# The expert weights of a dense loop in whole rows: two loads of 4096 bytes a partition instead of four of 2048

## The chip, the cores and the metric

The kernel runs on one core of a Trainium2 chip, in one launch. The metric is the device time of that launch in microseconds (us); of several runs the median is taken. The engines are TensorE (PE; its weight loads are listed as PEld), VectorE (DVE), ScalarE (ACT), GpSimd (POOL) and SyncE (SP); each works off its own list of instructions in a fixed order, and transfers are done by 16 DMA engines, which the instructions of SP and POOL feed.

## The reference

One decoder layer for 512 tokens of 1024 features: a sparse attention and a gated linear recurrence side by side, an output projection, LayerNorm, and then a layer that retrieves experts ("PEER"), LayerNorm again. The change lies in the PEER layer:

```python
def _peer(x, w_q, sub_keys, u, v):        # u, v: 16384 experts of 1024 floats each
    def one_block(xb):                    # 128 tokens
        q = (xb @ w_q).reshape(PEER_BLOCK, PEER_HEADS, 2, PEER_KEY_DIM // 2)
        s = jnp.einsum('thpd,hpkd->thpk', q, sub_keys).astype(jnp.float32)
        ...
        g = jax.nn.softmax(best, axis=-1).astype(xb.dtype)        # 8 heads, 16 experts each
        h = jax.nn.gelu(jnp.einsum('td,thkd->thk', xb, u[experts]))
        return jnp.einsum('thk,thkd->td', g * h, v[experts])
...
x = _layer_norm(ALPHA * h + ffn, ln2_g[layer], ln2_b[layer])
```

## The kernel before

The 512 tokens are four blocks of 128. Blocks 0 and 1 fetch the 128 experts of each token by indirect transfers (L627 on POOL, a ring `g` of four tiles, rows of 4096 bytes), and DVE multiplies and sums them (`gu` at L651, `gv` at L664). Blocks 2 and 3 ("dense") compute all 16384 experts for their 256 tokens, with a matrix `G` that holds each token's weight for each expert, zero for those not chosen.

`dense` first builds `G`: for four tokens at a time DVE writes two tiles of one-hot rows (`og`, L735), ACT multiplies the weights into one of them, PE multiplies the two (`gb`, L744) and ACT copies the product into `G` (L722). Then block 0 is finished: `finish(0)` does the LayerNorm of its accumulator in place (L143, L144) and stores it (L641).

The dense loop has 129 turns; turn j treats group j of 128 experts and the output side of group j - 1. In a step stand
- `into_hidden(j, n)`, for halves n = 0 and 1 of the features: a load of half of `u_j` (L767), and `split`: ACT rounds it to `u_nh` (L760), DVE subtracts to get the rest `u_nl` (L762); three times four matmuls add to `hp` (L771);
- `weigh`: the activation of `hp` gives `w` on ACT (L776), DVE multiplies in `G` (L777), then `wh` (ACT, L779) and `wl` (DVE, L781);
- `out_of_hidden(j - 1, n)`: a load of half of `v` (L786), `split` into `v_nh` and `v_nl`, and six matmuls for each half that add to `acc` (L791);
- `pump`: about two rows of experts of block 1 (one POOL transfer and one DVE instruction L651 or L664 each).

In turn 2, `residual` adds the layer's input to `acc` by 64 matmuls (L800); in turn 127, `finish(1)` ends block 1; after the loop the LayerNorm of blocks 2 and 3 and their store follow (L830).

The u halves have a ring of four tiles of 2 KB a partition, the v halves one of three, the split halves (`hl`) one of six. A load is issued by SP when its tile's last reader is done. The order of instructions on each engine is fixed when the program is built, by a scheduler that estimates when each could run; it is not the order of the text, and a change in tiles can move instructions of other engines.

Of the kernel before, what the change touches and what calls it, by code (L numbers as in the profile page):

```python
# [9 lines left out]
F32 = mybir.dt.float32  # L10
# [14 lines left out]
DENSE = (2, 3)  # L25
# buffers of the rings of tiles
HGB = 5
GB = 4
UB = 4
VB = 3  # L30
HLB = 6
# [3 lines left out]
# rows of experts worked off at each such place of the program (sel: one at every second step)  # L35
PUMP = {"cw": 4, "qi": 4, "hf": 4, "hq": 4, "hi": 4, "hg": 3, "qa": 2, "hgrn": 1, "att": 4, "mix": 1, "sel": 2,
        "q0": 7, "q1": 0, "q2": 0, "q3": 0}
# rows of block 0's sum that the tensor engine takes: after the queries, and beside the dense weights
# [4 lines left out]
# tokens of each four whose weights ScalarE multiplies in  # L43
GACTS = (3, 4)
# a row of experts at every so manyth group of the dense weights
GPUMP = 3
# the dense step by which all rows are worked off
# [4 lines left out]
def tile_decoder_layer(ctx, tc, a, out):  # L52
    nc = tc.nc

    cst = ctx.enter_context(tc.tile_pool(name="cst", bufs=1))
# [67 lines left out]
    def layer_norm(ys, os_, g, b, nm):  # L123
        """Each y is a tile or a list of its parts along the features."""
        n = len(ys)
        mv = cst.tile([128, n, 2], F32, name="mv" + nm, tag="ln_mv", bufs=2)
        parts = [y if isinstance(y, list) else [y[:, k * 512:(k + 1) * 512] for k in range(2)] for y in ys]
        for i in range(n):
            st = cst.tile([128, 2, 6], F32, name=f"st{nm}_{i}", tag="ln_st", bufs=2)
            for k in range(2):  # L130
                nc.vector.bn_stats(st[:, k, :], parts[i][k])  # L131
            nc.vector.bn_aggr(mv[:, i, :], st)
        ve = cst.tile([128, n], F32, name="ve" + nm, tag="ln_ve", bufs=2)
        nc.vector.tensor_scalar(ve, mv[:, :, 1], EPS, None, op0=ALU.add)
        r = rsqrt(ve, n, nm)
        for i, o in enumerate(os_):
            if isinstance(ys[i], list):
                for k in range(2):
                    sl = slice(k * 512, k * 512 + 512)
                    nc.vector.scalar_tensor_tensor(o[:, sl], parts[i][k], mv[:, i, 0:1], g[:, sl],  # L140
                                                   op0=ALU.subtract, op1=ALU.mult)
            else:
                nc.vector.scalar_tensor_tensor(o, ys[i], mv[:, i, 0:1], g, op0=ALU.subtract, op1=ALU.mult)  # L143
            nc.vector.scalar_tensor_tensor(o, o, r[:, i:i + 1], b, op0=ALU.mult, op1=ALU.add)  # L144
# [24 lines left out]
    hsA = cst.tile([128, 2, 1024], F32, name="hsA")  # L169
    hsB = cst.tile([128, 2, 1024], F32, name="hsB", tag="hsB")  # L170
    hTh = cst.tile([128, 8, 256], F32R, name="hTh")
    hs = [hsA[:, 0, :], hsA[:, 1, :], hsB[:, 0, :], hsB[:, 1, :]]
# [6 lines left out]
    def tok_major(blocks, xT, w, name):  # L179
        """x W for each block, tokens on partitions."""  # L180
# [12 lines left out]
    def feat_major(blocks, xT, w, name):  # L193
        """(x W)^T for all blocks at once, features on partitions: a bank for each 128 features."""
# [23 lines left out]
    def lower_bound():  # L218
# [7 lines left out]
        # lower bound of the forget gate: f = fa + fc * tanh(z / 2)  # L226
# [42 lines left out]
    def hgrn(b, pr, mixT):  # L269
# [42 lines left out]
        # the states before each chunk of 32  # L312
# [87 lines left out]
    def select(b, pr):  # L400
        """What to add to the negated attention scores of the keys that the index doesn't choose."""
# [91 lines left out]
    def queries(blocks, hT):  # L493
        """Sub-key scores and, for each of the 16 lists, its 16 best."""
# [54 lines left out]
    def best16(b, g, sv, si, bv, pos):  # L549
        # a pair (a, b) can be among the 16 best only if (a + 1) * (b + 1) <= 16; the places keep the pairs' order  # L550
# [16 lines left out]
    def routing(b, half, sv, si, bv, pos):  # L567
        """The experts and their weights for four of the block's heads."""
        H = slice(half * 4, half * 4 + 4)
        C = slice(half * 64, half * 64 + 64)  # L570
        # place -> the two ranks
# [22 lines left out]
        # rank -> sub-key  # L594
# [21 lines left out]
        # softmax over the 16 kept, whose first is their maximum  # L616
# [28 lines left out]
    def peer_gather(b):  # L645
        """Yields True after each row of experts is worked off, False where it waits for pe_gather."""
# [25 lines left out]
    def pe_gather(n, p):  # L672
        """A part of block 0's sum over the rows of v on the tensor engine: diag(weight) @ rows; yields after each."""
# [28 lines left out]
    def dense(den, dps):  # L702
        """Tokens of the DENSE blocks against every expert, with the experts' weights scattered to a dense matrix."""
# [4 lines left out]
        for i, b in enumerate(DENSE):  # L708
# [3 lines left out]
            t = den.tile([128, 4, 128], F32, name=f"dtr{b}", tag="v", bufs=VB)  # L712
            nc.scalar.copy(t[:, 0:3, :].rearrange("p a b -> p (a b)"), p[:, :384])
            tr[b] = [t[:, n, :] for n in range(3)]
# [13 lines left out]
        for t0 in range(0, T, 4):  # L728
# [3 lines left out]
            og = [den.tile([128, 4, 128], F32, name=f"og{t0}_{n}", tag=tag, bufs=bufs)  # L732
                  for n, (tag, bufs) in enumerate((("u", UB), ("hl", HLB)))]
# [30 lines left out]

        def into_hidden(j, n, hp):
            u = den.tile([128, 512], F32, name=f"u{j}_{n}", tag="u", bufs=UB)
            nc.sync.dma_start(u.rearrange("p (k i) -> p k i", k=4), a["ut"][j, :, n * 4:n * 4 + 4, :])  # L767
            uh, ul = split(f"u{j}_{n}", u)
# [15 lines left out]
        def out_of_hidden(j, n, wh, wl):  # L784
            v = den.tile([128, 512], F32, name=f"v{j}_{n}", tag="v", bufs=VB)
            nc.sync.dma_start(v, a["v"][j * 128:(j + 1) * 128, n * 512:(n + 1) * 512])  # L786
            vh, vl = split(f"v{j}_{n}", v)
# [15 lines left out]

        due = 0
# [124 lines left out]
```

## Time and profile before

| | |
|---|---|
| median of 3 runs | 1659.23 us (1658.19 to 1664.06) |
| span of the profiled execution, first to last instruction | 1647.0 us |
| its own time beside the span | not listed by itself; the median is 12.2 us above the span |
| PE busy | 1456.9 us (88%) |
| DVE busy | 1387.7 us (84%) |
| ACT busy | 706.5 us (43%) |
| POOL busy | 663.7 us (40%) |
| DMA moved | 467.89 MB, mean 284 GB/s |

The shares are means over the whole span. The building of `G` ends and the dense loop begins at about 880 us and the loop goes on to about 1634 us, so the loop is nearly half of the time. How the stages differ is in the rows below.

### The profile page before, as it was taken

How to read it: one execution, taken by the hardware profiler on the slowest of the kernel's cores; microseconds unless marked ns; L12 is line 12 of the kernel's file. 1: busy time of each engine (PE TensorE's matmuls, PEld its weight loads, DVE VectorE, ACT ScalarE, POOL GpSimd, SP SyncE). 2: the span in 40 equal slices, each digit the busy share in tenths (PEclk: the TensorE clock that was granted, in tenths of full speed). 3: DMA queues.
4: the chain of work that ended last, by engine and by line, in shares of the span. 5: the costliest groups of instructions: out<-in, count | busy, mean ns of one | idle time of the engine just before them, and what ended most of it. 6: DMA issues, size and time to landing. Idle time of an engine off the chain costs nothing. (4 is left out here: it accounts for less than half of the span.)

```text
span 1647.0 us, 24505 instructions
## 1 busy us (share of the span) xinstructions
PE 1456.9 (88%) x7858; PEld 1096.3 (67%) x7858; DVE 1387.7 (84%) x3263; ACT 706.5 (43%) x1501; POOL 663.7 (40%) x531
## 2 busy tenths in 40 slices
PE   8889899763577899868998999999999999999996
PEld 4567444542333365425667888888888889989885
DVE  4139899787787669998887899998999899999998
ACT  3312321122233010327996555555555555555553
POOL 0003423456665251135443344443444345534540
PEclk9899899755599999989999999999999999999998
DMA  7377878788887785246677999999999999999995
GB/s 284 122 275 248 280 265 290 245 273 275 262 276 252 264 306 186 84 136 226 220 218 263 327 345 351 355 345 344 343 356 344 336 347 359 365 349 345 354 358 191
DMA packets 166161, 467.89 MB, mean 284 GB/s; under 512 B 18576, under 2 KB 18704, under 8 KB 165904
## 3 DMA queue, kind: packets, MB, share of 16 engines
q0 software_dynamic: 73728, 268.47, 48.0%
q1 hardware_dynamic: 92304, 197.86, 33.2%
q8 instruction: 62, 1.02, 0.2%
q14 instruction: 67, 0.55, 0.1%
HBM read 464.16 MB, written 2.10 MB: 283 GB/s over the span
## 5 line engine op out<-in xcount | busy, mean ns | idle before, releaser
L627 POOL DMA_INDIRECT gv<-in_v_dram,idx x256 | 335.1, 1309 | 420.0 <-DVE hsA L664 268.6
L627 POOL DMA_INDIRECT gu<-in_u_dram,idx x256 | 318.6, 1245 | 458.2 <-DVE gu L651 289.3
L651 DVE SCALAR_TENSOR_TENSOR gu<-gu,hsA 128x1024 f32<-128x1024 f32 x256 | 309.5, 1225 | 52.5 <-DMA gu<-in_u_dram,idx 51.9
L664 DVE SCALAR_TENSOR_TENSOR hsA<-gv,gate,hsA 128x1024 f32<-128x1024 f32 x204 | 261.6, 1282 | 30.0 <-DMA gv<-in_v_dram,idx 26.6
L760 ACT CAST v_0h<-v 128x512 fp32r<-128x512 f32 x128 | 79.7, 622 | 96.7 <-PE acc L791 55.4
L518 PE MATMUL pq<-hT,wpq 128*128 128x128 f32 (+1 forms) x512 | 118.8, 390 | 0.0
L760 ACT CAST v_1h<-v 128x512 fp32r<-128x512 f32 x128 | 79.5, 621 | 88.6 <-DMA v<-in_v_dram 45.7
L762 DVE TENSOR_TENSOR u_0l<-u,u_0h 128x512 fp32r<-128x512 f32 x128 | 88.5, 692 | 32.7 <-ACT u_0h L760 29.9
L760 ACT CAST u_0h<-u 128x512 fp32r<-128x512 f32 x128 | 79.4, 620 | 72.2 <-PE hp L771 40.1
L791 PE MATMUL acc<-v_0h,wl 128*128 128x512 f32 x256 | 101.9, 398 | 2.5 <-DVE wl L781 2.5
L518 PEld LDWEIGHTS pq<-hT,wpq 128*128 128x128 f32 x512 | 80.0, 198 | 32.1 <-issue 1.7
L762 DVE TENSOR_TENSOR v_1l<-v,v_1h 128x512 fp32r<-128x512 f32 x128 | 87.8, 686 | 15.8 <-ACT v_1h L760 13.5
L791 PE MATMUL acc<-v_0h,wh 128*128 128x512 f32 x256 | 101.0, 394 | 0.0
L791 PE MATMUL acc<-v_1h,wl 128*128 128x512 f32 x256 | 99.7, 389 | 0.0
L791 PE MATMUL acc<-v_1h,wh 128*128 128x512 f32 x256 | 99.7, 389 | 0.0
L791 PE MATMUL acc<-v_0l,wh 128*128 128x512 f32 x256 | 99.5, 390 | 0.0
L760 ACT CAST u_1h<-u 128x512 fp32r<-128x512 f32 x128 | 79.4, 621 | 46.4 <-PE acc L791 42.3
L735 DVE TENSOR_TENSOR og<-iota,dtr 128x512 f32<-128x512 f32 x128 | 81.6, 687 | 13.6 <-PE gb L744 11.7
L762 DVE TENSOR_TENSOR u_1l<-u,u_1h 128x512 fp32r<-128x512 f32 x128 | 87.8, 686 | 5.1 <-ACT wh L779 2.7
L762 DVE TENSOR_TENSOR v_0l<-v,v_0h 128x512 fp32r<-128x512 f32 x128 | 88.0, 688 | 3.4 <-ACT v_0h L760 2.1
L682 PE MATMUL pw<-gv,dg 128*128 128x512 f32 x152 | 76.0, 623 | 15.6 <-ACT dg L680 9.1
L771 PE MATMUL hp<-hTl,u_0h 128*128 128x256 f32 x512 | 84.3, 287 | 5.8 <-ACT u_0h L760 5.8
(282 smaller groups left out, 3166.6 us busy)
## 6 DMA issues: line engine op xcount, KB each, us to landing
v<-in_v_dram SPq DMA_DIRECT2D x256, 256.0 KB
u<-in_ut_dram SPq DMA_DIRECT2D x256, 256.0 KB
wpq<-in_w_pq_dram SPq DMA_DIRECT2D x32, 512.0 KB
wo<-in_w_o_dram SPq DMA_DIRECT2D x16, 512.0 KB
hfw<-in_w_hf_dram SPq DMA_DIRECT2D x8, 512.0 KB
hqw<-in_w_hq_dram SPq DMA_DIRECT2D x8, 512.0 KB
hiw<-in_w_hi_dram SPq DMA_DIRECT2D x8, 512.0 KB
qaw<-in_w_qa_dram SPq DMA_DIRECT2D x8, 512.0 KB
```

The costliest lines, as they stand in the source:

```text
L518: nc.tensor.matmul(qp[:, :nt], w[:, k, :], hT[:, k, :nt], start=(k == 0), stop=(k == 7))
L627: nc.gpsimd.indirect_dma_start(out=t, out_offset=None, in_=table, in_offset=bass.IndirectOffsetOnAxis(ap=idx[b][k // 64][:, k % 64:k % 64 ...
L651: nc.vector.scalar_tensor_tensor(g, g, 1.0, hs[b], op0=ALU.mult, op1=ALU.mult, accum_out=hd[:, k:k + 1]))
L664: nc.vector.scalar_tensor_tensor(hs[b], g, gate[:, b, k:k + 1], hs[b], op0=ALU.mult, op1=ALU.add))
L682: nc.tensor.matmul(p[i], dg, g[:, i * 512:(i + 1) * 512], start=(k == ks[0]), stop=(k == ks[-1]))
L735: nc.vector.tensor_tensor(og[n], iota[:, None, :].to_broadcast([128, 4, 128]), x[n][:, c:c + 4, None].to_broadcast([128, 4, 128]), op=ALU. ...
L760: nc.scalar.copy(h, x)
L762: nc.vector.tensor_tensor(l, x, h.bitcast(F32), op=ALU.subtract)
L771: nc.tensor.matmul(hp, ut[:, k * 128:(k + 1) * 128], ht[:, n * 4 + k, :], start=(n + q + k == 0), stop=(n == 1 and q == 2 and k == 3))
L791: nc.tensor.matmul(acc[i][n], wt[:, sl], vt, start=(j == 0 and q == 0), stop=(j == 127 and q == 2))
```

## The change

The two rings for u and v halves become one ring `uv` of three tiles of 4 KB a partition, and one load brings the whole of `u_j` or `v_j`. A fourth 4 KB tile is `hs0`, the tile in which block 0's input, sum and result lie (the tile `hsA` of before held blocks 0 and 1 and is now two tiles): every fourth load, which is u2, u4, u6 and so on, goes there. Both halves of a tile come free together, when the last of the four splitting instructions has read it. While `G` is built, the tables of both dense blocks (`dtr`) take one tile of the ring, and the first one-hot tiles, now for eight tokens at once, the other two.

```diff
-UB = 4
-VB = 3
+UVB = 3
...
-    hsA = cst.tile([128, 2, 1024], F32, name="hsA")
+    hs0 = cst.tile([128, 1024], F32, name="hs0", tag="hs0")
+    hs1 = cst.tile([128, 1024], F32, name="hs1")
...
-            t = den.tile([128, 4, 128], F32, name=f"dtr{b}", tag="v", bufs=VB)
-            nc.scalar.copy(t[:, 0:3, :].rearrange("p a b -> p (a b)"), p[:, :384])
-            tr[b] = [t[:, n, :] for n in range(3)]
+            if not tr:
+                t = den.tile([128, 8, 128], F32, name="dtr", tag="uv", bufs=UVB)
+            nc.scalar.copy(t[:, 3 * i:3 * i + 3, :].rearrange("p a b -> p (a b)"), p[:, :384])
+            tr[b] = [t[:, 3 * i + n, :] for n in range(3)]
...
-            og = [den.tile([128, 4, 128], F32, name=f"og{t0}_{n}", tag=tag, bufs=bufs)
-                  for n, (tag, bufs) in enumerate((("u", UB), ("hl", HLB)))]
+            if t0 % 8 == 0:
+                og8 = den.tile([128, 8, 128], F32, name=f"og{t0}", tag="uv", bufs=UVB)
+            og = [og8[:, t0 % 8:t0 % 8 + 4, :], den.tile([128, 4, 128], F32, name=f"og{t0}_1", tag="hl", bufs=HLB)]
...
+        loaded = []
+
+        def load_rows(nm, src):
+
+            if len(loaded) % 4 == 3:
+                t = cst.tile([128, 1024], F32, name=nm, tag="hs0")
+            else:
+                t = den.tile([128, 1024], F32, name=nm, tag="uv", bufs=UVB)
+            nc.sync.dma_start(t, src)
+            loaded.append(nm)
+            return t
+
         def into_hidden(j, n, hp):
-            u = den.tile([128, 512], F32, name=f"u{j}_{n}", tag="u", bufs=UB)
-            nc.sync.dma_start(u.rearrange("p (k i) -> p k i", k=4), a["ut"][j, :, n * 4:n * 4 + 4, :])
-            uh, ul = split(f"u{j}_{n}", u)
+            if n == 0:
+                cur["u"] = load_rows(f"u{j}", a["ut"][j].rearrange("p k i -> p (k i)"))
+            uh, ul = split(f"u{j}_{n}", cur["u"][:, n * 512:(n + 1) * 512])
...
         def out_of_hidden(j, n, wh, wl):
-            v = den.tile([128, 512], F32, name=f"v{j}_{n}", tag="v", bufs=VB)
-            nc.sync.dma_start(v, a["v"][j * 128:(j + 1) * 128, n * 512:(n + 1) * 512])
-            vh, vl = split(f"v{j}_{n}", v)
+            if n == 0:
+                cur["v"] = load_rows(f"v{j}", a["v"][j * 128:(j + 1) * 128, :])
+            vh, vl = split(f"v{j}_{n}", cur["v"][:, n * 512:(n + 1) * 512])
```

The instructions of PE, DVE and ACT are the same in number and kind; SP has 386 rows instead of 642. The order on the engines changes from the building of `G` on. Three places follow.

SP at the start of the dense loop, before; the number ahead of the last one in a name like `u3_1_6159` is the half, `out_0_dram<-hsA` is the store of block 0:

```order
L786 DMA v1_1_6110<-in_v_dram 128x512
L767 DMA u3_1_6159<-in_ut_dram 128x512
L786 DMA v2_0_6147<-in_v_dram 128x512
L767 DMA u4_0_6197<-in_ut_dram 128x512
L786 DMA v2_1_6184<-in_v_dram 128x512
L767 DMA u4_1_6233<-in_ut_dram 128x512
L786 DMA v3_0_6221<-in_v_dram 128x512
L641 DMA out_0_dram<-hsA_104 128x1024
L767 DMA u5_0_6271<-in_ut_dram 128x512
L786 DMA v3_1_6258<-in_v_dram 128x512
L767 DMA u5_1_6309<-in_ut_dram 128x512
```

SP at the same place after the change, where `u3_6081` is the whole of u3 and `hs0` is block 0's tile:

```order
L775 DMA u0_5862<-in_ut_dram 128x1024
L775 DMA u1_5907<-in_ut_dram 128x1024
L775 DMA v0_5931<-in_v_dram 128x1024
L775 DMA v1_6001<-in_v_dram 128x1024
L775 DMA u3_6081<-in_ut_dram 128x1024
L775 DMA v2_6105<-in_v_dram 128x1024
L641 DMA out_0_dram<-hs0_104 128x1024
L775 DMA u2_5977<-in_ut_dram 128x1024
L775 DMA u4_6151<-in_ut_dram 128x1024
L775 DMA v3_6175<-in_v_dram 128x1024
L775 DMA u5_6221<-in_ut_dram 128x1024
```

The store has moved ahead of u2, u4 and v3, and u2 goes into the tile that it reads.

PE around the end of step 98, before; `u98_1l` is DVE's part of u98's second half, and "x4" are four matmuls:

```order
L791 MATMUL acc1_1_5892<-v97_1h_13180,wl97_13102 128x512
L791 MATMUL acc1_1_5892<-v97_1h_13180,wh97_13100 128x512
L771 MATMUL hp99_13190<-hTl_4549,u99_0h_13193 128x256 x4
L771 MATMUL hp99_13190<-hTh_106,u99_0h_13193 128x256 x4
L791 MATMUL acc0_1_5890<-v97_1l_13182,wh97_13100 128x512
L791 MATMUL acc1_1_5892<-v97_1l_13182,wh97_13100 128x512
L771 MATMUL hp99_13190<-hTh_106,u99_0l_13195 128x256 x4
L771 MATMUL hp99_13190<-hTl_4549,u99_1h_13229 128x256 x4
L771 MATMUL hp99_13190<-hTh_106,u99_1h_13229 128x256 x4
L771 MATMUL hp99_13190<-hTh_106,u99_1l_13231 128x256 x4
L791 MATMUL acc0_0_5889<-v98_0h_13217,wl98_13176 128x512
```

PE at the same place after the change:

```order
L805 MATMUL acc1_1_5860<-v97_1h_12754,wl97_12682 128x512
L805 MATMUL acc1_1_5860<-v97_1h_12754,wh97_12680 128x512
L785 MATMUL hp98_12694<-hTh_107,u98_1l_12733 128x256 x4
L805 MATMUL acc0_1_5858<-v97_1l_12756,wh97_12680 128x512
L805 MATMUL acc1_1_5860<-v97_1l_12756,wh97_12680 128x512
L785 MATMUL hp99_12764<-hTl_4550,u99_0h_12767 128x256 x4
L785 MATMUL hp99_12764<-hTh_107,u99_0h_12767 128x256 x4
L785 MATMUL hp99_12764<-hTh_107,u99_0l_12769 128x256 x4
L785 MATMUL hp99_12764<-hTl_4550,u99_1h_12801 128x256 x4
L785 MATMUL hp99_12764<-hTh_107,u99_1h_12801 128x256 x4
L785 MATMUL hp99_12764<-hTh_107,u99_1l_12803 128x256 x4
L785 MATMUL hp100_12834<-hTl_4550,u100_0h_12837 128x256 x4
```

Before, all of hp98 stood ahead of the twelve `acc` matmuls of v97 (its end is above these rows), and hp99 was followed by the `acc` of v98; now the four matmuls with `u98_1l` stand behind ten of the twelve, and hp99 and the start of hp100 follow each other.

DVE in steps 98 and 99, before; `L664` is a row of block 1's experts:

```order
L664 SCALAR_TENSOR_TENSOR hsA_104<-gv1_74_13135,gate_111,hsA_104 128x1024
L777 TENSOR_TENSOR w97_13097<-w97_13097,G_4716 128x256
L762 TENSOR_TENSOR v97_0l_13145<-v97_0_13141,v97_0h_13143 128x512
L664 SCALAR_TENSOR_TENSOR hsA_104<-gv1_75_13138,gate_111,hsA_104 128x1024
L762 TENSOR_TENSOR u98_1l_13157<-u98_1_13153,u98_1h_13155 128x512
L781 TENSOR_TENSOR wl97_13102<-w97_13097,wh97_13100 128x256
L762 TENSOR_TENSOR v97_1l_13182<-v97_1_13178,v97_1h_13180 128x512
L762 TENSOR_TENSOR u99_0l_13195<-u99_0_13191,u99_0h_13193 128x512
L664 SCALAR_TENSOR_TENSOR hsA_104<-gv1_76_13209,gate_111,hsA_104 128x1024
L777 TENSOR_TENSOR w98_13171<-w98_13171,G_4716 128x256
L762 TENSOR_TENSOR v98_0l_13219<-v98_0_13215,v98_0h_13217 128x512
L664 SCALAR_TENSOR_TENSOR hsA_104<-gv1_77_13212,gate_111,hsA_104 128x1024
```

DVE in the same steps after the change:

```order
L791 TENSOR_TENSOR w97_12677<-w97_12677,G_4716 128x256
L664 SCALAR_TENSOR_TENSOR hs1_105<-gv1_75_12716,gate_112,hs1_105 128x1024
L764 TENSOR_TENSOR v97_0l_12723<-v97_12719,v97_0h_12721 128x512
L795 TENSOR_TENSOR wl97_12682<-w97_12677,wh97_12680 128x256
L764 TENSOR_TENSOR u98_1l_12733<-u98_12695,u98_1h_12731 128x512
L764 TENSOR_TENSOR v97_1l_12756<-v97_12719,v97_1h_12754 128x512
L764 TENSOR_TENSOR u99_0l_12769<-u99_12765,u99_0h_12767 128x512
L664 SCALAR_TENSOR_TENSOR hs1_105<-gv1_76_12783,gate_112,hs1_105 128x1024
L764 TENSOR_TENSOR v98_0l_12793<-v98_12789,v98_0h_12791 128x512
L791 TENSOR_TENSOR w98_12747<-w98_12747,G_4716 128x256
L664 SCALAR_TENSOR_TENSOR hs1_105<-gv1_77_12786,gate_112,hs1_105 128x1024
L764 TENSOR_TENSOR u99_1l_12803<-u99_12765,u99_1h_12801 128x512
```

Of u98, wl97 and v97, `wl97` has moved ahead of `u98_1l`; one step later `wl98` stands behind `v98_1l`.

## Rows read from the trace of the kernel before

**Rows 1.** The page's first line: the span and the instructions.

```profile
span 1647.0 us, 24505 instructions
```

**Rows 2.** Windows: length; busy PE, PEld, DVE, ACT, POOL; clock, DMA share, GB/s.

```profile
1000.00:1600.00 600.00, 593.08 (x3744) 534.25 (x3743) 556.29 (x887) 322.21 (x628) 275.86 (x191) 1.00 0.97 350
...
880.00:890.00 10.00, 7.96 (x47) 7.97 (x48) 6.39 (x13) 6.14 (x9) 3.27 (x3) 0.66 0.66 212
...
800.00:850.00 50.00, 47.27 (x247) 32.42 (x246) 43.30 (x79) 50.00 (x126) 22.67 (x21) 1.00 0.73 230
```

**Rows 3.** Waits from 850 to 1640: total us, times, longest.

```profile
ACT v_1h L760 <- DMA v<-in_v_dram: 45.7, 42, 2.2
...
ACT v_0h L760 <- DMA v<-in_v_dram: 21.0, 19, 2.0
```

**Rows 4.** Timeline, DVE: `u_0l` of steps 9, 17, 25, 31, 34, 36, 70, 76, 78, 94.

```profile
940.00 0.69 DVE L762 TENSOR_TENSOR u_0l<-u,u_0h 128x512 fp32r<-128x512 f32 x1 [0.15 <-ACT u_0h L760]
...
986.93 0.69 DVE L762 TENSOR_TENSOR u_0l<-u,u_0h 128x512 fp32r<-128x512 f32 x1 [0.38 <-ACT u_0h L760]
...
1032.62 0.69 DVE L762 TENSOR_TENSOR u_0l<-u,u_0h 128x512 fp32r<-128x512 f32 x1 [0.15 <-ACT u_0h L760]
...
1067.09 0.69 DVE L762 TENSOR_TENSOR u_0l<-u,u_0h 128x512 fp32r<-128x512 f32 x1 [0.15 <-ACT u_0h L760]
...
1084.37 0.69 DVE L762 TENSOR_TENSOR u_0l<-u,u_0h 128x512 fp32r<-128x512 f32 x1
...
1097.20 0.68 DVE L762 TENSOR_TENSOR u_0l<-u,u_0h 128x512 fp32r<-128x512 f32 x1
...
1295.58 0.69 DVE L762 TENSOR_TENSOR u_0l<-u,u_0h 128x512 fp32r<-128x512 f32 x1 [0.40 <-ACT u_0h L760]
...
1331.48 0.69 DVE L762 TENSOR_TENSOR u_0l<-u,u_0h 128x512 fp32r<-128x512 f32 x1
...
1343.16 0.69 DVE L762 TENSOR_TENSOR u_0l<-u,u_0h 128x512 fp32r<-128x512 f32 x1
...
1433.29 0.69 DVE L762 TENSOR_TENSOR u_0l<-u,u_0h 128x512 fp32r<-128x512 f32 x1
```

**Rows 5.** Timeline from 1364 to 1374, five rows of two plain steps.

```profile
1364.04 0.68 DVE L762 TENSOR_TENSOR u_1l<-u,u_1h 128x512 fp32r<-128x512 f32 x1
...
1364.97 0.68 DVE L762 TENSOR_TENSOR v_1l<-v,v_1h 128x512 fp32r<-128x512 f32 x1
...
1370.71 0.62 ACT L760 CAST u_0h<-u 128x512 fp32r<-128x512 f32 x1 [0.80 <-PE hp L771]
...
1372.35 0.62 ACT L760 CAST v_0h<-v 128x512 fp32r<-128x512 f32 x1 [0.73 <-PE acc L791]
...
1373.74 0.52 PE L771 MATMUL hp<-hTl,u_0h 128*128 128x256 f32 x3
```

**Rows 6.** DMA queues from 1000 to 1600: packets, MB, share of 16 engines.

```profile
q1 hardware_dynamic: 59978, 109.21, 50.0%
...
q0 software_dynamic: 27426, 99.87, 46.9%
```

**Rows 7.** Timeline at the start of the dense loop, five engines' rows.

```profile
876.65 3.19 SPq L767 DMA_DIRECT2D u<-in_ut_dram  x3
...
881.36 0.62 ACT L760 CAST u_0h<-u 128x512 fp32r<-128x512 f32 x1 [2.21 <-DMA u<-in_ut_dram]
...
895.39 0.42 DVE L777 TENSOR_TENSOR w<-w,G 128x256 f32<-128x256 f32 x1
...
900.19 0.48 PE L791 MATMUL acc<-v_0h,wl 128*128 128x512 f32 x1
...
900.77 1.28 DVE L144 SCALAR_TENSOR_TENSOR hsA<-hsA,rs_yl,ln 128x1024 f32<-128x1024 f32 x1
```

**Rows 8.** Timeline at the end of the dense loop, PE and SP.

```profile
1631.69 0.50 PE L791 MATMUL acc<-v_0h,wl 128*128 128x512 f32 x1 [1.54 <-DVE wl L781]
...
1641.76 1.53 SPq L830 DMA_DIRECT2D out_dram<-y  x2
```

More of the change, by code (lines that the diff above doesn't have):

```diff
@@ L168, in tile_decoder_layer @@
     kiT = pre.tile([128, 512], F32, name="kiT")
-    hsA = cst.tile([128, 2, 1024], F32, name="hsA")
+    hs0 = cst.tile([128, 1024], F32, name="hs0", tag="hs0")
+    hs1 = cst.tile([128, 1024], F32, name="hs1")
     hsB = cst.tile([128, 2, 1024], F32, name="hsB", tag="hsB")
     hTh = cst.tile([128, 8, 256], F32R, name="hTh")
-    hs = [hsA[:, 0, :], hsA[:, 1, :], hsB[:, 0, :], hsB[:, 1, :]]
+    hs = [hs0, hs1, hsB[:, 0, :], hsB[:, 1, :]]
     idx = [[cst.tile([128, 64], U32, name=f"idx{b}_{n}") for n in range(2)] for b in range(2)]
@@ L802, in residual @@
                                              start=False, stop=False)
+        cur = {}
         due = 0
```

## The prediction

> **What bounds the kernel now.** I read the page first, then the windows, the waits of the dense loop, single steps on the timeline, and the two ends of the loop. The span is 1647.0 us [rows 1]; the median of the three runs is 1659.23, so 12.2 us lie around the span, and I carry them over unchanged.
>
> The windows show where the change works: from 1000 to 1600 PE is busy 593.08 of 600 us, DVE 556.29, the DMA share is 0.97 and the granted clock 1.00 [rows 2]. TensorE sets the pace, DVE has some 7% to spare and DMA almost nothing, so an edit matters if it makes PE wait, and an edit that only saves issues does not. One step of the dense loop is 24 matmuls of `hp` and 12 of `acc`. Its price is read from the distance of the `u_0l` subtractions, one per step (step 0 is the first). That distance depends on the order in which the engines go through a step [rows 4]:
> - plain order (DVE ends a step with u1, wl, v1; step 78 to 94): 90.13 us / 16 = 5.63;
> - crossed order (wl ahead of u1 in one step, behind v1 in the next; PE runs two `hp` in a row and takes the last four of one behind the `acc`; step 70 to 76): 35.90 / 6 = 5.98, 0.35 over plain;
> - alternating order (wl first, then v1 first, with two rows of experts a step; step 9 to 17): 46.93 / 8 = 5.87, 0.24 over;
> - a step that already takes in the next step's w ("knot"; step 25 to 31): 34.47 - 6 x 5.63 = 0.7 for each knot.
>
> The waits say what the loads do today: ACT waits for v 42 times at the second half and 19 times at the first, 66.7 us in total [rows 3], and no list entry of size stands for u. Most of it is hidden behind ACT's idle half. Where it shows, as in steps 34 and 35, two steps took 12.83 us, 1.6 over plain [rows 4]; I find two more such places (steps 42 and 122), so late v costs about 3.5 us of the whole.
>
> **The change, part by part.** *256 issues fewer.* Three issues in a row take SP 3.19 us with the gaps between them [rows 7]; SP has nothing else to do in the loop, so the saving is worth nothing on the path.
>
> *Bytes.* The same bytes in rows of 4096 instead of 2048. Between 1000 and 1600 the loads (2048-byte rows) moved 109.21 MB for 50.0% of the engines' time, the gathers (4096-byte rows) 99.87 MB for 46.9% [rows 6]: 0.458 against 0.470 per MB. Longer rows cost no less per byte. The Trainium skill's page "DMA: Bandwidth & Descriptors", section "Rules for kernel authors", asks for transfers of at least 1 MiB and for many small ones to be joined into a large one; by that rule the loads get cheaper. The trace does not agree at these sizes, and the measurement decides: I put the DMA time at unchanged.
>
> *How early a load may start.* v is as before: a tile is free when v1 of two steps earlier has been subtracted (1365.66), and the cast of v_0 comes at 1372.35: 6.7 us [rows 5]. Only the second half now comes with the first, and the late second halves go: -3.5 us (0 to -4). For u the tiles were freed by halves, the first of them by u_0l, which opens a step on DVE. Now the whole load waits for u_1l of two steps earlier, 1364.04 + 0.68, and the cast comes at 1370.71: this leaves 6.0 us [rows 5] for twice the bytes. v with its 6.7 is late 61 times in 256 today, so u will be late too. What catches it: the cast ends at 1371.33 and PE takes u_0h at 1373.74, 2.4 us later [rows 5]; behind the cast on ACT stands w, which DVE takes about 1.5 us after it. A load 1.5 us late costs nothing. Bounds: 0 and, if each load comes 7.5 to 8 us after its issue, 0.2 a step in every step, 25 us. I take +2, because the nearest rows (late v) are mostly hidden.
>
> *Order of the steps.* The instructions are the same, their order is not; the excerpts show steps 98 and 99, plain before and crossed now. Counting the crossed steps in both orders: 17 before (59 to 75), after 6 (58 to 63), 12 (77 to 88) and 19 (96 to 114). In steps 39 to 56 the alternating order replaces three knots. So 18 x 0.24 - 3 x 0.7 = +2.2; (6 - 17) x 0.35 = -3.9; 31 x 0.35 = +10.9, less two knots of before (95, 114), +9.5. Sum +7.8; bounds 0 (if DVE's spare time hides the crossing there) and +11.
>
> *Start of the loop.* u2 now goes into `hs0`, the tile from which block 0's result is stored. So SP issues: store of `hs0`, then u2, which waits for the store to have landed, and every later load (u4, v3, u5) stands behind u2. Before, the store stood behind u4 and v3 and nothing waited for it. Today the last LayerNorm row starts at 900.77 and takes 1.28 [rows 7]. After, DVE takes it right behind w of step 1, which stands at 895.39 now and will stand at about the same time (PE goes through hp0 and hp1 without hp2 and the last of G between them, but begins some 1.3 us later, an estimate: today's u_0 is issued at 876.65 and cast at 881.36 [rows 7], and u0 is twice as large). So LayerNorm ends about 897. The two final stores of the kernel bound a store: issued from 1641.76 for 1.53 us, span end 1647.0 [rows 1, 8], 3.7 to 5.2 us. u2 is issued at about 902 and comes no sooner than u0's 4.7 us later, about 907, and its cast about 0.7 later. PE has by then hp0, hp1, v0's twelve and half of the residual behind it, ends them about 900.5, and has nothing else in its order. At 900.19 of today [rows 7] it had done that and 12 matmuls of hp2 (1.4 us). Lag: 907.5 - 900.2 + 1.4 = 8.7. When PE stood idle ahead of 882, the stretch 880 to 890 was granted 0.66 [rows 2], part of it at the lower of the two levels; a longer idle time brings the like again, +1.5. Start: +10, between +5 (store and load at their short ends, LayerNorm two us earlier) and +13. The other side, no loss, is a rival.
>
> *G stage.* The one-hot tiles for eight tokens at once share two free 4 KB tiles. From 800 to 850 ACT is busy 50.00 of 50 [rows 2]; it hides what DVE and the ring do, 0. Without that cover DVE would be next, with 43.30 of 50 and the same work as before.
>
> *End of the loop.* Today PE waits 1.54 us for wl of step 127 [rows 8], because the last u_1l matmuls stand behind the acc of step 126 and w behind a late v half. After, they stand ahead of it: -1.5 (0 to -3).
>
> Sum: -3.5 + 2 + 7.8 + 10 + 0 - 1.5 = +14.8; 1659.2 + 14.8 = **1674**.
>
> **Rivals.** *A, no measurable change (1657 to 1667).* The stall at u2 is short, because LayerNorm comes about 893 and store and load take 3.7 and 4 us (+4), and DVE's spare time absorbs half of the crossing (+4). For it: the price of crossed steps was read where DVE was busiest. Against it: u2's two waits in a row are in the order, and nothing but the order differs between the crossed stretch and the plain one next to it. About 1662.
>
> *B, faster.* Late v sets more of the steps than I see: what looks like the price of an order is the price of a late half. With no late halves every step falls towards 5.63. From step 9 (940.00) to 94 (1433.29) the loop takes 493.29 us for 85 steps, 5.80 [rows 4]; 0.17 less over 118 steps is 20 us, and with the start's +10 the time is about 1649. It decides as soon as the crossed steps come at 5.65. For it: 66.7 us of waits. Against it: plain steps wait for v too and hold 5.63.
>
> A rule of the Trainium skill lies on this side: the same page, "DMA: Bandwidth & Descriptors", "Queues, rings and completion order", says that a DMA engine goes round the queues packet by packet. As a mechanism of this kernel: beside the gathers' rows of 4096 bytes, a load's rows of 2048 would get a third of the bytes while both queues are full, and rows of 4096 a half; loads would land sooner, in favour of B. The traces so far show no landing time by row size, so I add it to B's chance and not to the sum.
>
> *C, much slower.* u is the bound. Two tiles serve two steps; a tile is held from the cast to the end of u_1l, 11.2 - 6.0 = 5.2 us, so a step cannot be shorter than (landing time + 5.2) / 2. With 1.5 us of slack it decides from about 7.5 us; at 8 us a plain step becomes 5.85, and some 60 of them add 13, the other steps about a third of that: 1659 + 15 + 18 = 1692. For it: DMA at 0.97, and v's lateness with 6.7. Against it: when steps lengthen, DMA has less to do and lands sooner.
>
> *D, the loads are not halved.* The order shows 386 rows on SP instead of 642; I leave this out.
>
> **How the numbers follow.** The forecast gets 0.48 (1667 to 1684 alone), A 0.25, B 0.08, C 0.19. The bound of what a measurement can tell is 0.5%, 8.3 us: faster is under 1651, slower over 1667.5. B gives faster 0.07; A with the rest gives same 0.26; slower 0.67. Leaving out half of B and half of C, the range is 1656 to 1692.
>
> **What would show it.** In the profile after: on SP u2 issued about 902, and a wait of PE or ACT for DMA u of 5 to 7 us near 900 to 907; if this wait is under 2 us, the start was wrong. The distance of `u_0l` in steps 78 to 88 and 97 to 113 about 5.98 a step; if 5.65, the order's price was wrong. ACT's waits for v below 30 us, and waits for u of 10 to 60 us; if PE's waits for u_0h sum to over 20 us in the loop, C holds. The G stage as long as before.

## The result and the profile after

The changed kernel takes 1698.05 us (median of 6 runs, 1690.89 to 1706.22) against 1659.88 for the kernel before on the same chip: the ratio is 1.0249, with a 95% interval of 1.022 to 1.0279. It is slower by 38 us, 24 above the forecast time and 6 above the range. In this and every later run a launch is 1.7 to 2.0 us longer than its profiled span; so some 10 of the 12.2 us between median and span of the kernel before are the scatter of its executions, and not time around the span.

The page of the profiled execution, its span and the two busiest engines, against [rows 1]:

```profile
span 1692.7 us, 23882 instructions
## 1 busy us (share of the span) xinstructions
PE 1471.5 (87%) x7858; PEld 1098.5 (65%) x7858; DVE 1387.4 (82%) x3263; ACT 707.4 (42%) x1501; POOL 657.0 (39%) x531
```

The busy times are those of before to about 1%; what grew is idle time. The window from 1000 to 1600, where [rows 2] had PE at 593.08 us and a DMA share of 0.97:

```profile
1000.00:1600.00 600.00, 574.41 (x3553) 510.53 (x3552) 527.44 (x851) 306.90 (x594) 243.39 (x181) 1.00 0.92 332
```

PE lost 19 us there at full clock, and DMA was less busy, not more. The waits from 915 to 1680 say for what (total us, times, longest), against [rows 3]:

```profile
ACT u_0h L762 <- DMA u<-in_ut_dram: 61.2, 40, 3.9
ACT v_0h L762 <- DMA v<-in_v_dram: 46.3, 44, 2.4
...
PE hp L785 <- ACT u_0h L762: 12.2, 20, 2.2
PE hp L785 <- DVE u_1l L764: 11.8, 25, 0.9
```

The late second halves of v are gone, as forecast, but u, which was never late in the loop, is now late 40 times, and PE waits for what comes of it. One such step on the timeline (SP's issue of a u, the cast of it, PE's first use):

```profile
1486.96 0.33 SPq L775 DMA_DIRECT2D u<-in_ut_dram  x1
...
1493.78 0.62 ACT L762 CAST u_0h<-u 128x512 fp32r<-128x512 f32 x1 [1.32 <-DMA u<-in_ut_dram]
...
1494.45 0.74 PE L785 MATMUL hp<-hTl,u_0h 128*128 128x256 f32 x4 [0.46 <-ACT u_0h L762]
```

The load is issued as soon as its tile is free (`u_1l` ends at 1486.93), and its cast starts 6.8 us later, where the prediction had 6.0; PE waits 0.46 us. The step is a crossed one: the same timeline of DVE shows `wl` behind `v_1l` in it. The loop from step 4 to step 127 is the distance of these two rows of `u_0l`, 745.29 us:

```profile
924.31 0.69 DVE L764 TENSOR_TENSOR u_0l<-u,u_0h 128x512 fp32r<-128x512 f32 x1 [0.69 <-ACT u_0h L762]
...
1669.60 0.64 DVE L764 TENSOR_TENSOR u_0l<-u,u_0h 128x512 fp32r<-128x512 f32 x1
```

In the kernel before it was 711.73:

```profile
911.29 0.69 DVE L762 TENSOR_TENSOR u_0l<-u,u_0h 128x512 fp32r<-128x512 f32 x1 [0.70 <-ACT u_0h L760]
...
1623.02 0.68 DVE L762 TENSOR_TENSOR u_0l<-u,u_0h 128x512 fp32r<-128x512 f32 x1
```

So 33.6 us of the loss lie in the steady loop. At its start the wait for the store is there as forecast (store, u2 with u4 behind it, the cast of u2, PE; against [rows 7]):

```profile
901.21 0.35 SPq L641 DMA_DIRECT2D out_dram<-hs  x1
...
906.47 8.38 SPq L775 DMA_DIRECT2D u<-in_ut_dram  x2
...
909.65 0.62 ACT L762 CAST u_0h<-u 128x512 fp32r<-128x512 f32 x1 [9.41 <-DMA u<-in_ut_dram]
...
910.32 1.22 PE L785 MATMUL hp<-hTl,u_0h 128*128 128x256 f32 x4 [4.78 <-ACT u_0h L762]
```

From step 0 to step 4 the loop takes 34.07 us (890.23 to 924.31) instead of 29.28 (882.01 to 911.29), 4.8 more. From step 127 to the end of the span it is 23.1 instead of 24.0. The sum, 4.8 + 33.6 - 0.9 = 37.5, comes near the measured loss of 38.2. The two profiled spans differ by more, 45.7, because step 0 came 8.2 us later. I put that down to scatter: step 0 came between 880.1 and 894.9 in the 16 kernels profiled here, and at 882.0, 891.9, 880.4 and 891.6 in those with half tiles, so that the profiled execution of before was an early one.

### The profile page after: what moved, and what is told of

It is laid out like the page before. It is cut to its first block, busy times and chain, and to the rows that moved or that the text cites. A ratio compares the mean times of both kernels' runs of the same rounds, so it can differ in the third digit from the quotient of the medians.

```text
span 1692.7 us, 23882 instructions
## 1 busy us (share of the span) xinstructions
PE 1471.5 (87%) x7858; PEld 1098.5 (65%) x7858; DVE 1387.4 (82%) x3263; ACT 707.4 (42%) x1501; POOL 657.0 (39%) x531
## 5 line engine op out<-in xcount | busy, mean ns | idle before, releaser
L627 POOL DMA_INDIRECT gv<-in_v_dram,idx x256 | 329.2, 1286 | 445.4 <-DVE hs L664 297.7
L651 DVE SCALAR_TENSOR_TENSOR gu<-gu,hs 128x1024 f32<-128x1024 f32 x256 | 309.6, 1224 | 54.9 <-DMA gu<-in_u_dram,idx 52.3
L664 DVE SCALAR_TENSOR_TENSOR hs<-gv,gate,hs 128x1024 f32<-128x1024 f32 x204 | 261.5, 1282 | 33.5 <-DMA gv<-in_v_dram,idx 32.2
L762 ACT CAST v_0h<-v 128x512 fp32r<-128x512 f32 x128 | 79.6, 622 | 103.7 <-DMA v<-in_v_dram 46.3
L785 PE MATMUL hp<-hTh,u_1l 128*128 128x256 f32 x512 | 86.1, 290 | 12.8 <-DVE u_1l L764 11.8
L785 PEld LDWEIGHTS hp<-hTl,u_0h 128*128 128x128 f32 x512 | 75.8, 190 | 32.8 <-ACT u_0h L762 25.7
```

The costliest lines, as they stand in the source:

```text
L627: nc.gpsimd.indirect_dma_start(out=t, out_offset=None, in_=table, in_offset=bass.IndirectOffsetOnAxis(ap=idx[b][k // 64][:, k % 64:k % 64 ...
L651: nc.vector.scalar_tensor_tensor(g, g, 1.0, hs[b], op0=ALU.mult, op1=ALU.mult, accum_out=hd[:, k:k + 1]))
L664: nc.vector.scalar_tensor_tensor(hs[b], g, gate[:, b, k:k + 1], hs[b], op0=ALU.mult, op1=ALU.add))
L762: nc.scalar.copy(h, x)
L785: nc.tensor.matmul(hp, ut[:, k * 128:(k + 1) * 128], ht[:, n * 4 + k, :], start=(n + q + k == 0), stop=(n == 1 and q == 2 and k == 3))
```

## The experiments

Theory 1: u is late, because its whole tile comes free only with u_1l; theory 2: the order of the steps costs the time; theory 3: rows of 4096 bytes slow the transfers. The ratio of each time to that of the kernel before on the same chip, and the loop from step 4 to 127 of one profiled execution of each. "Plain order" means that VectorE's six instructions of a step are held in it; the rows of experts and the other engines' instructions are still placed by the scheduler:

| run | ratio, 95% interval | step 4 to 127, us |
|---|---|---|
| before | 1 | 711.7 |
| changed kernel | 1.0249 (1.022 to 1.0279) | 745.3 |
| e1 five tiles | 1.0088 (1.0061 to 1.0115) | 719.6 |
| e2 two halves | 1.0178 (1.0143 to 1.0213) | 732.0 |
| e3 hs0 later | 1.0287 (1.0249 to 1.0325) | 755.7 |
| e4 before, 3 u tiles | 1.0063 (1.0042 to 1.0084) | 720.4 |
| e5 changed, plain order | 1.0062 (1.0032 to 1.0092) | 719.5 |
| e6 before, plain order | 0.9957 (0.9933 to 0.9981) | 702.6 |
| e7 two by partition | 1.1741 (1.1672 to 1.1811) | 983.5 |
| e8 five tiles, plain, hs0 later | 0.9883 (0.984 to 0.9926) | 696.3 |
| e9 e5 in two halves | 1.0 (0.9975 to 1.0025) | 704.8 |
| e10 e9, second half first | 1.0288 (1.0208 to 1.0367) | 757.4 |
| e11 before, plain, 4 v tiles | 0.9968 (0.9942 to 0.9995) | 708.6 |
| e12 e5, hs0 later | 1.0078 (1.0043 to 1.0112) | 721.6 |
| e13 e8 with the store's wait | 0.9921 (0.9898 to 0.9944) | 696.2 |
| e14 e8 in two halves | 0.9925 (0.9896 to 0.9953) | 695.8 |

**e1, one more tile.** Two of its 4 KB come from `wl`, which moves to tiles of `cst` that are free by then.

```diff
-UVB = 3
+UVB = 4
...
-            if len(loaded) % 4 == 3:
+            if len(loaded) % 5 == 4:
```

> The changed kernel with one more 4 KB tile: whole loads of u and v go round five tiles (four of the ring and hs0 as every fifth) instead of four, so a load may be issued half a step earlier (about 2.8 us more than 6.0). The step order keeps many alternating and crossed steps (about as many as in the changed kernel). Theory 1 (u comes late because its whole tile is freed only by u_1l): ACT's waits for u and v in the loop fall from about 107 us to under 30, the time falls by 20 to 30 us, to about 1670. Theory 2 (the order of the steps costs it): the waits fall but the time stays within 8 us of 1698. Theory 3 (rows of 4096 bytes slow the transfers): both stay.

The loop falls by 25.7 us, ACT waits for u not at all, and for v 13.6 us once at the start (now v1 waits for the store) and 4.2 us in the loop:

```profile
ACT v_0h L763 <- DMA v<-in_v_dram: 17.8, 5, 13.6
```

Theory 1 holds for this much, and theory 3 falls. Theory 2 alone falls only as far as the orders are alike, for the scheduler has placed some of the steps otherwise than in the changed kernel. And 7.9 us more than before remain in a loop almost without late loads.

**e2, each load in two.**

```diff
-            nc.sync.dma_start(t, src)
+            for n in range(2):
+                nc.sync.dma_start(t[:, n * 512:(n + 1) * 512], src[:, n * 512:(n + 1) * 512])
```

> The changed kernel, each load of 4096 bytes a partition issued as two of 2048 into the two halves of the same tile; ring, release and order of the steps as in the changed kernel. Theories 1 and 2: within 6 us of the changed kernel, 1692 to 1704. Theory 3: the length of the rows is what matters, and the time falls by more than 10 us, below 1688.

Faster by some 12 us than the changed kernel: what theory 3 expected, though in another order of some steps, and two causes are possible (shorter rows, or the first half landing by itself). e7, e9 and e10 were made for that.

**e3, hs0 first for u4.**

```diff
-            if len(loaded) % 4 == 3:
+            if len(loaded) % 4 == 3 and len(loaded) > 3:
```

> The changed kernel, but hs0 is first used for u4 and not for u2, so that u2 does not wait for the store of block 0's result. The order of the later steps is the same. If the stall at u2 is worth what the trace shows (u_0h waits 9.4 us for u2, 5 to 6 us of it a lag of the loop), the time falls by 4 to 8 us, to about 1692; if the lag is made up later, or the wait only moves to u4, it stays within 3 us of 1698.

The lag is gone (27.59 us from step 0 to 4), but the loop takes 10.4 us more and the time does not fall. The order of the loop is the changed kernel's but for a few instructions, so 10 us is also what the loops of two executions with late loads can differ by. Not settled by this run.

**e4, before with three u tiles.**

```diff
-UB = 4
+UB = 3
```

> The kernel before with three u half tiles of 2 KB instead of four, nothing else: rows of 2048 bytes, halves freed apart; a u half then waits for the half three earlier. The order is the plain one in nearly all steps, with the crossed steps 59 to 75 gone. Theory 1: u comes late here too, ACT waits for u 20 us or more, and the time rises by 8 to 25 us, to 1668 to 1685. Theory 2: with fewer crossed steps the time falls by about 5 us, to 1655. Theory 3: no change beyond that, 1655 to 1660.

Slower by 0.63%, 10 us, with 33.9 us of ACT's waits for u where there were none, although its order has more plain steps: theory 1, with rows of 2048 bytes.

**e5, the changed kernel in the plain order.** `at` holds the instructions by name; the added edges only fix VectorE's order.

```diff
...
+        seq = []
+        for j in range(4, 126):
+            seq += [at[n] for n in (f"u{j}_0", f"w{j - 1}", f"v{j - 1}_0", f"u{j}_1", f"wl{j - 1}", f"v{j - 1}_1")]
+        for x, y in zip(seq, seq[1:]):
+            tc.add_manual_dep(y, x.name, mybir.DependencyInfo(mybir.DependencyClass.NoSync, mybir.DependencyReason.DATA), reason="order")
```

> The changed kernel with VectorE's six instructions of a step held in the plain order (u0, w, v0, u1, wl, v1) from step 4 to 125; rings and loads as in the changed kernel. Theory 1: the cycle of u's tile (landing 6.6 us, held 5.2 us, two tiles for two steps) sets about 5.9 us a step whatever the order, so the time falls by less than 10 us, to 1688 to 1698. Theory 2 (the order): every step falls towards 5.65 and the time falls by 25 to 35 us, to about 1668.

PE's and ACT's order change along with it. The time falls by 31 us and the loop by 25.8: theory 2's number, although the loads are as late as before, in sum later:

```profile
ACT v_0h L764 <- DMA v<-in_v_dram: 90.0, 81, 2.8
ACT u_0h L764 <- DMA u<-in_ut_dram: 49.6, 41, 2.3
```

So theory 1 as I had sharpened it, a cycle that sets the step whatever the order, is wrong. Either remedy, one more tile or the plain order, takes away about the same 26 us.

**e6, before in the plain order** (the same edit).

> The kernel before with VectorE's six instructions of a step held in the plain order from step 4 to 125; half tiles and loads as before. If the order's prices read from its trace are right (0.35 crossed, 0.24 alternating, 0.7 a knot), the loop falls from 712 us for steps 4 to 127 to about 697, and the time by 10 to 17 us, to about 1642. If the late v halves set those steps, it falls by less than 5 us.

The loop falls by 9.2 us and the time by 0.43%, 7 us, less than the 10 to 17 expected. The late v remains in full:

```profile
ACT v_1h L762 <- DMA v<-in_v_dram: 41.9, 41, 2.0
ACT v_0h L762 <- DMA v<-in_v_dram: 15.1, 16, 1.8
```

**e7, each load in two of 64 partitions.**

```diff
-            nc.sync.dma_start(t, src)
+            for n in range(2):
+                nc.sync.dma_start(t[n * 64:(n + 1) * 64, :], src[n * 64:(n + 1) * 64, :])
```

> The changed kernel, each load issued as two of 64 partitions with rows of 4096 bytes: as many and as large transfers as in e2, but each half of the features needs both. If e2 gained because the first half of the features lands by itself, this one gains nothing: 1692 to 1704. If e2 gained because smaller transfers land sooner, about as e2: 1680 to 1688.

17% slower, neither of the two. The window from 1000 to 1600 and its DMA queues (packets, MB, share):

```profile
1000.00:1600.00 600.00, 487.05 (x2724) 421.06 (x2723) 409.19 (x679) 226.67 (x458) 177.72 (x139) 0.93 1.02 255
```

```profile
q1 hardware_dynamic: 24280, 79.58, 54.3%
q0 software_dynamic: 19945, 72.62, 46.8%
```

The DMA engines are full with 255 GB/s: 0.68% of their time for a MB of loads, and 0.64% for one of the unchanged gathers, against 0.44% and 0.48% in the changed kernel (below). This form has a cost of its own and tells nothing of e2.

**e8, whole loads at their best:** e1's ring, hs0 first for the tenth load, plain order.

```diff
+            if len(loaded) % 5 == 4 and len(loaded) > 5:
```

> Whole loads at their best: five tiles as in e1, hs0 first used by the tenth load, so that no load waits for the store, and VectorE in the plain order. Theory 1 with the order's prices: loads on time, plain steps at 5.65, no stall: 1638 to 1648, within 6 us of e6. If rows of 4096 bytes cost something of their own (theory 3), it stays over 1655.

The fastest of all, 1.2% under the kernel before (1634.64 us against 1652.74, 19 runs), and 10 us under e6, where at most 6 were expected. The window from 1000 to 1600, and the one wait for a load that is left in the loop:

```profile
1000.00:1600.00 600.00, 599.73 (x3826) 543.58 (x3825) 570.19 (x908) 323.18 (x641) 259.92 (x196) 1.00 0.97 357
```

```profile
ACT v_0h L765 <- DMA v<-in_v_dram: 2.8, 3, 1.2
```

PE is busy 599.73 of 600 us, and every ten steps from 4 to 124 run at 5.64 to 5.69 a step.

**e9, e5 with each load in two,** e2's edit.

> e5 (changed kernel, plain order) with each load issued as two of 2048 bytes a partition, first half first, as in e2, but with the same order of the steps as e5. If e2 gained from the loads and not from its slightly other order, ACT's waits for u and v (139.6 us in e5) fall below 90 and the time falls by 6 to 14 us, to about 1652. If e2 gained from its order, no change: 1658 to 1667.

The order is e5's but for a few instructions, and the two issues of a load follow each other, so that both halves still wait for the whole tile. The gain is 14.8 us in the loop and 0.6% in the time: most of e2's gain came from the loads. The waits for the first halves fall from 139.6 us to 60.9:

```profile
ACT v_0h L764 <- DMA v<-in_v_dram: 48.1, 41, 2.5
ACT u_0h L764 <- DMA u<-in_ut_dram: 12.8, 11, 2.1
```

**e10, the second half first.**

```diff
+            for n in (1, 0):
```

> e9 with the second half of each row issued ahead of the first: as many, as large and as long transfers, but the half that is cast first is issued last. If e9 gains because the first half lands by itself, this one gains nothing over e5: 1658 to 1670. If smaller transfers or shorter rows land sooner, as e9.

The same transfers in the other sequence, in nearly the same order of steps: the loop is 52.7 us longer than in e9, and 38 longer than with one whole load:

```profile
ACT u_0h L764 <- DMA u<-in_ut_dram: 86.7, 52, 3.3
ACT v_0h L764 <- DMA v<-in_v_dram: 68.8, 57, 4.5
```

That it is worse than e5, and not equal, I had not expected, and why stays open. For the question it is enough: neither the length of the rows nor the number of loads made e9 faster; what is left is that the half that is cast first arrives by itself.

**e11, before in the plain order with four v tiles** (`VB = 4`, room as in e1).

> The kernel before in the plain order with four v half tiles instead of three (the 2 KB a partition come from wl, which moves to tiles that are free by then): half loads, but early. If depth alone makes e8 faster than e6, this one comes to e8: 1632 to 1641. If whole loads have a gain of their own, it stays near e6: 1643 to 1648.

ACT has no wait for v left, yet the time stays at e6's. VectorE's order is not quite the plain one here (in pairs of steps a row of experts stands on the other side of `w` or of `wl`), and PE waits 7.2 us for u_1l. Inconclusive on the value of whole rows, which is why e14 was made; but it shows that a loop without late loads, VectorE's six instructions in the plain order, can still take 708.6 us where e8 takes 696.3.

**e12, e5 with hs0 first for u4,** e3's edit.

> e5 with hs0 first used for u4 instead of u2, as in e3, in the plain order. If the stall at u2 is a lag that stays, the time falls by 4 to 8 us from e5, to about 1657. If the loop gives it back, as e3 suggested, it stays within 3 us of 1663.

From step 0 to 4 it takes 28.02 us instead of e5's 36.59, from step 4 to 127 2.1 more; the time does not fall, but runs of these kernels lie 20 us apart.

**e13, e8 with the store's wait** (`if len(loaded) % 5 == 4:`).

> e8 with hs0 already the fifth load's tile (v1), which then waits for the store of block 0; else the same, order included but for a few rows. Loads are on time later, so nothing else moves. If a lag at the start stays to the end, the time is 8 to 11 us over e8 (ratio to before 0.993 to 0.996); if the loop makes it up, within 3 us of e8 (0.986 to 0.990).

From step 0 to 4 it takes 39.71 us instead of 28.02, 11.7 more, and the rest of the loop is the same to 0.1 us. The ratios differ by 0.0038, 6 us (with the intervals of both, -2 to 14), which lies between the two outcomes expected. In the profiled execution the lag of the start stays to the end; the times alone do not decide.

**e14, e8 with each load in two.**

> e8 with each load issued as two of 2048 bytes a partition; the order hardly changes. If a ring of five is deep enough either way, the time is that of e8 within 3 us, and rows of 4096 bytes and half as many issues are worth nothing by themselves. If longer rows make the transfers cheaper, e14 is over 5 us slower than e8.

The loop is the same to 0.4 us. The time is 7 us longer, with intervals that overlap (0.9896 to 0.9953 against 0.984 to 0.9926). The profiled spans differ by 11.0 us, and none of it lies in steps 4 to 127: 6.1 ahead of step 0, 1.5 from there to step 4, and 3.8 behind step 127, where a row of block 1's LayerNorm stands ahead of VectorE's last instructions and PE waits for `wl`:

```profile
1630.35 0.56 PE L809 MATMUL acc<-v_0h,wl 128*128 128x512 f32 x1 [2.17 <-DVE wl L799]
```

For the loop I read it as no difference; whether the time differs is open.

## Why the prediction was wrong

The side was right (slower, chance 0.67), the size was not: +14.8 forecast, +38 measured.

**Two terms of the sum were mis-sized**, both far too small; the start of the loop, put 5 us too high, hid some of it. The four kernels of e5, e6 and the originals, with e1 and e8 as the loop with hardly a late load, split the 33.6 us of the loop:

| step 4 to 127, us | its order | plain order | the order costs |
|---|---|---|---|
| before, half tiles | 711.7 | 702.6 | 9.2 |
| after, whole loads, four tiles | 745.3 | 719.5 | 25.8 |
| whole loads, five tiles | 719.6 (e1) | 696.3 (e8) | 23.4 |

The plain column is read from these rows of `u_0l`, steps 4 and 127 of e6, e5 and e8, and then e9:

```profile
911.36 0.69 DVE L764 TENSOR_TENSOR u_0l<-u,u_0h 128x512 fp32r<-128x512 f32 x1 [0.70 <-ACT u_0h L762]
...
1613.92 0.69 DVE L764 TENSOR_TENSOR u_0l<-u,u_0h 128x512 fp32r<-128x512 f32 x1
```

```profile
924.52 0.69 DVE L766 TENSOR_TENSOR u_0l<-u,u_0h 128x512 fp32r<-128x512 f32 x1 [0.69 <-ACT u_0h L764]
...
1644.02 0.68 DVE L766 TENSOR_TENSOR u_0l<-u,u_0h 128x512 fp32r<-128x512 f32 x1
```

```profile
916.44 0.69 DVE L767 TENSOR_TENSOR u_0l<-u,u_0h 128x512 fp32r<-128x512 f32 x1 [0.69 <-ACT u_0h L765]
...
1612.70 0.64 DVE L767 TENSOR_TENSOR u_0l<-u,u_0h 128x512 fp32r<-128x512 f32 x1
```

```profile
922.34 0.69 DVE L766 TENSOR_TENSOR u_0l<-u,u_0h 128x512 fp32r<-128x512 f32 x1 [0.70 <-ACT u_0h L764]
...
1627.10 0.67 DVE L766 TENSOR_TENSOR u_0l<-u,u_0h 128x512 fp32r<-128x512 f32 x1
```

*How early a load may start.* The step that failed is "A load 1.5 us late costs nothing", on which the +2 rests; with "the late second halves go: -3.5" it gave -1.5. Measured in the plain order, e5 against e6, it is 719.5 - 702.6 = +16.9. The place was right, and so was the lateness: in the changed kernel late u came 61.2 / 40 = 1.5 us late on average, late v 46.3 / 44 = 1.1. A whole load took about 1 us longer than a half (median from issue to landing at the end of each row, from 1000 to 1600; the halves are e4's, the whole loads e3's):

```profile
u<-in_ut_dram SPq DMA_DIRECT2D x206, 256.0 KB, 5.8
v<-in_v_dram SPq DMA_DIRECT2D x206, 256.0 KB, 6.1
```

```profile
u<-in_ut_dram SPq DMA_DIRECT2D x98, 512.0 KB, 6.6
v<-in_v_dram SPq DMA_DIRECT2D x98, 512.0 KB, 7.3
```

Such lateness is not free. e9 keeps e5's ring, release and order and lets the first half land by itself: ACT's waits fall by 78.7 us and the loop by 14.8. So most of the 16.9 is the joint landing; the 2.2 us between e9 and e6 are left for the joint release and what else differs. The 2.4 us between the cast of u_0 and PE did not cover it, because u_0 is not the only cast that is late. In e5 PE never waits for `u_0h`; it waits for the second half of u:

```profile
PE hp L787 <- DVE u_1l L766: 8.4, 14, 1.2
PE hp L787 <- ACT u_1h L764: 6.1, 10, 1.1
```

All ten waits for `u_1h` come within 3.5 us of a late `v_0h`, whose cast stands ahead of u_1's on ACT. Of the 14 waits for `u_1l`, 13 have no late load that near, and e11, without late loads, also has 14 of them, 7.2 us; their cause is not shown to be the loads.

*Order of the steps.* Forecast +7.8 (0 to +11), measured 25.8 - 9.2 = +16.6. That the scheduler would make more of the dear steps was right, and theory 2's test (e5) shows the order as a cause of its own. The price of a crossed step was right too: in e1, where ACT's waits for loads sum to 1.7 us between steps 78 and 113, the plain steps 78 to 88 come at 5.65 and the crossed steps 97 to 113 at 6.01 (first and last `u_0l` of each stretch):

```profile
1363.83 0.69 DVE L765 TENSOR_TENSOR u_0l<-u,u_0h 128x512 fp32r<-128x512 f32 x1
...
1420.35 0.69 DVE L765 TENSOR_TENSOR u_0l<-u,u_0h 128x512 fp32r<-128x512 f32 x1
...
1471.70 0.69 DVE L765 TENSOR_TENSOR u_0l<-u,u_0h 128x512 fp32r<-128x512 f32 x1 [0.65 <-ACT u_0h L763]
...
1567.91 0.69 DVE L765 TENSOR_TENSOR u_0l<-u,u_0h 128x512 fp32r<-128x512 f32 x1 [1.01 <-ACT u_0h L763]
```

The totals were off on both sides. By the prediction's prices the order of the kernel before cost some 15 us (712 to 697 in what was expected of e6; measured 9.2), and the changed kernel's 7.8 more, some 23 (measured 25.8). In the changed kernel, with its late loads, steps 78 to 88 and 97 to 113 came at 6.31 and 6.16, where 5.98 was forecast.

*How sure the split is.* The two terms give the 33.6 us by construction. That they are separate causes is seen in the table: one more tile saves 25.7 us in the scheduler's order and 23.2 in the plain one, though e1's order is not quite the changed kernel's. That each remedy alone gives about 26 us does not make them one cause. The sizes are rougher. Each loop is one execution, and holding six instructions does not hold the rest: between e5, e6 and e8, 67 to 150 of VectorE's 1108 instructions of the steps stand elsewhere, most of them rows of experts. What that can be worth show e11 and e14, both with halves and hardly a late load: 708.6 and 695.8. So the price of late v in the kernel before, 702.6 - 696.3 = 6.3 at face value, is not shown. By the times of whole launches, with the start of the loop taken off, the loads are worth about 12 us and the order about 25. Either way both terms lie far above the -1.5 and +7.8 of the forecast.

*Start of the loop.* Forecast +10, seen in the trace +4.8 from step 0 to 4. The store landed 5.3 us after its issue, u2 came 3.2 us after its own (I had 4.7), and PE waited 4.78 us for it, where the lag was put at 8.7. A kernel that never lets u2 wait is 6.5 (e3) or 8.6 us (e12) shorter there. That such a lag stays to the end is shown in e13's trace; in e3 and e12 the times do not show it, and why e3's loop was 10 us longer stays open.

*Bytes.* Forecast no change. With loads on time, a MB of whole rows took 0.441% of the engines' time and one in halves 0.461%, e8 and e14 from 1000 to 1600:

```profile
q1 hardware_dynamic: 30607, 111.43, 49.1%
```

```profile
q1 hardware_dynamic: 61094, 111.26, 51.3%
```

So longer rows are 4% cheaper, against my reading of two different streams in [rows 6]; but PE was busy all the time in e8, and the loop of e14 is no longer. This is the side of the Trainium skill's rule ("DMA: Bandwidth & Descriptors", "Rules for kernel authors") to join small transfers into large ones. In the changed kernel a MB of loads got cheaper and one of gathers dearer (0.44% and 0.48%, against 0.458 and 0.470 in [rows 6]), but in e8 and e14 gathers took 0.46% beside either length, and a whole load still came later than a half (e3 and e4 above). The Trainium skill's rule on taking turns by packet ("DMA: Bandwidth & Descriptors", "Queues, rings and completion order"), which the prediction put on the side of B, is neither shown nor refuted by that. The rows of the changed kernel:

```profile
q0 software_dynamic: 26219, 95.47, 46.3%
q1 hardware_dynamic: 28360, 103.26, 45.6%
```

*Issues, G stage, end of the loop.* Nothing gained by fewer issues, as forecast; the start of the loop lies where it lay, within its scatter; PE's wait for the last wl fell from 1.54 to 0.27 us and the end by 0.9 (forecast 1.5).

*Rivals.* A fell: the crossed stretches came at 6.31 and 6.16 a step, and PE waited at the start. B had one thing right: without late loads every plain step comes at 5.65 (e8); but the change made loads later, not earlier. C had the right place, late loads behind tiles that come free late, and they are a third to a half of the loss; its formula, a cycle of u's two tiles that sets the step, fell with e5, where v was late more often than u. By the sign that was to mean C, PE's waits for `u_0h` over 20 us, it would have been missed: they sum to 12.2.

## What to carry to other kernels

Joining two loads into one takes away two freedoms at once, the first half's early landing (14.8 us here) and the first half's early release; before doing it, take the time from "tile free" to "first use" and compare it with the landing time of the joined load, not of the halves. If the ring can't be made deeper, leave the halves apart; with one tile more, it made no difference to the loop here. A change of tiles also moves a scheduler's order: hold the good order by hand first, and then compare rings; here holding it was worth 26 us to one loop and 9 to the other, and whole loads with a fifth tile, the held order and no wait for the store beat the kernel before by 1.2% (e8).

## What was unexpected of the hardware

Two transfers of 64 partitions in place of one of 128, same rows, same bytes, cost 54% more DMA time per MB (0.68% against 0.44%), and the gathers beside them, which were unchanged, 33% more (e7). The sequence of two halves in one queue decided over 52.7 us of a loop (e9, e10). Late loads did not come with fuller DMA engines: in the changed kernel the moved rate fell from 350 to 332 GB/s at a busy share of 0.92, and in e8, almost without late loads, it rose to 357 at 0.97. An engine that is busy about half of the time still passed lateness on: ACT was busy 312 of 600 us in e5, and 78.7 us less of its waits for loads went with a loop 14.8 us shorter (e5, e9).
